# Linear attention with a relu feature map: output product turned round, with KV as the stationary operand and a transpose back in fp32

## Chip, cores, metric

One core of a Trainium2 chip. The metric is the device time of one execution in microseconds (us); several executions are taken of each kernel, each kernel beside the kernel before on the same chip. The span in a profile is shorter than the time by about 1.8 us, because it runs from the first to the last recorded instruction.

## The reference

```python
# Q, K, V: (8, 12, 512, 64) fp32
Q_feat = np.maximum(0, Q);  K_feat = np.maximum(0, K)
KV    = np.einsum('bhkd,bhkv->bhdv', K_feat, V)
K_sum = np.sum(K_feat, axis=2)
numerator   = np.einsum('bhqd,bhdv->bhqv', Q_feat, KV)
denominator = np.einsum('bhqd,bhd->bhq', Q_feat, K_sum)
return numerator / (denominator[:, :, :, None] + 1e-10)
```

There are 96 heads. The kernels take K and V in 24 groups of four heads and Q and the output in 12 "octets" of eight. Inputs are 37.7 MB, the output 12.6 MB.

## The kernel before

K, V and Q come in as bf16 (cast by the transfer). VectorE applies relu and head masks to K, V is masked by VectorE and ScalarE in halves, TensorE makes KV with the sum of K in a 65th column, ScalarE copies KV to SBUF as a block-diagonal pair of heads. Q is transposed on TensorE and put through relu by ScalarE into two buffers, padded with zeros, so that each 32-column strip of the array works for one pair of heads. The output product then has Q as the stationary operand and comes out with rows on the partitions, ready to be divided by its own 65th column.

```python
def mm_kv(g):
    ps_kv[g] = pkv.tile([P, 2, D1], fp32, name="ps_kv")          # pkv: 2 PSUM buffers
    for r in range(R):                                           # R = 16
        nc.tensor.matmul(ps_kv[g], kf[g][:, r, :, :]..., vo[g % NB][:, r, :, :],
                         start=(r == 0), stop=(r == R - 1), ...)
# ... cut ...
def mm_out(o, j):                                                # rounds of 6, 6 and 4
    # ... cut ...
    for v in range(nu):
        for z in range(2):
            for w in range(4):                                   # four 32-column strips
                nc.tensor.matmul(po[hs, b, c:c + 2 * D1],
                    qtf[o % NZ][:, z, u * P + 32 * w:u * P + 32 * w + 32],
                    kvd[(2 * o + h // 4) % NK][:, h % 4 // 2, h % 2, :, :], start=(z == 0), stop=(z == 1), ...)

def norm(o, j, o_sb):
    nc.vector.tensor_scalar(den, pv[:, :, :, D], scalar1=1e-10, scalar2=None, op0=Alu.add)
    nc.vector.reciprocal(rec, den)
    nc.vector.tensor_tensor(o_sb[...], pv[:, :, :, 0:D], rec.unsqueeze(3).to_broadcast(...), op=Alu.mult)

def cuts(o):                                                     # stores of octets 1 and 3 in pieces
    return ((16, P), (0, 5), (5, 10), (10, 15), (15, 16)) if o in (1, 3) else ((0, P),)
# ... cut: one loop over octets interleaves kv, out_round of the octet before, preparation, qt and store
```

Stores are held back on purpose: the queue that issues them first reads a bit of a K tile five octets ahead.

Of the kernel before, what the change touches and what calls it, by code (L numbers as in the profile page):

```python
# [10 lines left out]
def kernel(  # L11
# [7 lines left out]
    nc = tc.nc  # L19
    B, H, S, D = Q.shape  # L20
    assert D == 64
    P = 128
    D1 = D + 1
# [3 lines left out]
    R = S * 4 // P  # L27
    RQ = S * 8 // P
    NHG = 4
    U = RQ // 2  # L30
    NG = NH // NHG
    NO = NG // 2
# [4 lines left out]
    fp32 = mybir.dt.float32  # L37
# [4 lines left out]
    def pool(name, bufs, **kw):  # L42
        return ctx.enter_context(tc.tile_pool(name=name, bufs=bufs, **kw))
# [5 lines left out]
    kfp = pool("kfp", 4)  # L49
    rcp = pool("rcp", 4)  # L50
    outp = pool("outp", DELAY + 2)
    pkv = pool("pkv", 2, space=bass.MemoryType.PSUM)
    pqt = pool("pqt", 2, space=bass.MemoryType.PSUM)
    pou = pool("pou", 2, space=bass.MemoryType.PSUM)

    def view(X, f):
# [2 lines left out]
    Qr, Kr, Vr, Or = view(Q, RQ * D), view(K, R * D), view(V, R * D), view(out, RQ * D)  # L59

    ident = consts.tile([P, P], bf16, name="ident")
    NB = 4
    NK = 4
    NZ = 2




    vo = [consts.tile([P, R, 2, D1], bf16, name=f"vo{i}") for i in range(NB)]
    kvf = [consts.tile([P, NHG * 2 * D1], bf16, name=f"kvd{i}") for i in range(NK)]  # L70
    kvd = [x.rearrange("p (t s c d) -> p t s c d", t=2, s=2, c=2) for x in kvf]
    mask = consts.tile([P, 2, 2], fp32, name="mask")
    scratch = consts.tile([1, D], bf16, name="scratch")


    qtf = [consts.tile([P, 2, U * P], bf16, name=f"qt{i}") for i in range(NZ)]
    qtz = [x.rearrange("p z (u w y c) -> p z u w y c", u=U, w=4, y=2) for x in qtf]

    ctx.enter_context(tc.manual_schedule())

# [17 lines left out]
        nc.scalar.dma_start(out=v_sb[g].rearrange("p r d -> p (r d)"), in_=Vr[g])  # L98
    load_q(0)
    make_identity(nc, ident)  # L100
    for o in range(1, NO):
        load_kv(2 * o)
        load_kv(2 * o + 1)
        load_q(o)

    def zero(i):
        if i == 0:
            for h in range(NHG):
                for s in range(2):
                    nc.vector.memset(mask[32 * h:32 * h + 32, 0, s:s + 1], 1.0 if h % 2 == s else 0.0)  # L110
            for t in range(2):
                nc.vector.memset(mask[:, 1, t:t + 1], 0.0)
                nc.vector.memset(mask[64 * t:64 * t + 64, 1, t:t + 1], 1.0)
        if i < NB:
            nc.vector.memset(vo[i][:, :, :, D:D1], 0.0)
            for t in range(2):
                nc.vector.memset(vo[i][64 * t:64 * t + 64, :, t, D:D1], 1.0)
        nc.vector.memset(kvf[i].bitcast(fp32), 0.0)  # L118

    def zero_q(i):  # L120
        nc.vector.memset(qtf[i].rearrange("p z f -> p (z f)").bitcast(fp32), 0.0)  # L121

    kf, ps_kv, ps_qt, ps_out = {}, {}, {}, {}

    def prep(g):
        kf[g] = kfp.tile([P, R, 2, D], bf16, name="kf")
        for s in range(2):
            nc.vector.tensor_scalar(kf[g][:, :, s, :], k_sb[g], scalar1=0.0,  # L128
                                    scalar2=mask[:, 0, s:s + 1], op0=Alu.max, op1=Alu.mult)
        nc.vector.tensor_scalar(vo[g % NB][:, :, 0, 0:D], v_sb[g], scalar1=mask[:, 1, 0:1],  # L130
                                scalar2=None, op0=Alu.mult)

    def prep_act(g):
        nc.scalar.activation(vo[g % NB][:, :, 1, 0:D], v_sb[g], Act.Copy, scale=mask[:, 1, 1:2])  # L134

    def mm_kv(g):
        ps_kv[g] = pkv.tile([P, 2, D1], fp32, name="ps_kv")
        for r in range(R):
            nc.tensor.matmul(  # L139
                ps_kv[g], kf[g][:, r, :, :].rearrange("p s d -> p (s d)"), vo[g % NB][:, r, :, :],  # L140
                start=(r == 0), stop=(r == R - 1), skip_group_check=True)

    def evac_kv(g):
        for s in range(2):
            for c in range(2):
                nc.scalar.copy(kvd[g % NK][64 * c:64 * c + 64, :, s, c, :],  # L146
                               ps_kv[g][64 * s:64 * s + 64])


    def transp(o, i):  # L150
        ps_qt[o, i] = pqt.tile([P, U // 2, P], bf16, name="ps_qt")
        for u in range(U // 2):
            nc.tensor.transpose(ps_qt[o, i][:, u, :], q_sb[o][:, i * (U // 2) + u, :], ident)  # L153

    def evac_qt(o, i, eng=None):
        us = slice(i * (U // 2), (i + 1) * (U // 2))
        pv = ps_qt[o, i].rearrange("p u (w y c) -> p u w y c", w=4, y=2)
        for z in range(2):
            if eng is nc.vector:
                eng.tensor_scalar(qtz[o % NZ][:, z, us, :, z, :], pv[:, :, :, z, :], scalar1=0.0,  # L160
                                  scalar2=None, op0=Alu.max)
            else:
                nc.scalar.activation(qtz[o % NZ][:, z, us, :, z, :], pv[:, :, :, z, :], Act.Relu)  # L163


    ROUNDS = ((0, 6), (6, 6), (12, 4))

    def mm_out(o, j):
        po = pou.tile([P, 2, 512], fp32, name="ps_out")
        ps_out[o, j] = po  # L170
        u0, nu = ROUNDS[j]
        for v in range(nu):
            u, b, c = u0 + v, v // (nu // 2), v % (nu // 2) * 2 * D1
            for z in range(2):
                for w in range(4):
                    hs = slice(32 * w, 32 * w + 32)
                    h = 2 * w + z
                    nc.tensor.matmul(  # L178
                        po[hs, b, c:c + 2 * D1],
                        qtf[o % NZ][:, z, u * P + 32 * w:u * P + 32 * w + 32],  # L180
                        kvd[(2 * o + h // 4) % NK][:, h % 4 // 2, h % 2, :, :],
                        start=(z == 0), stop=(z == 1), skip_group_check=True)

    def norm(o, j, o_sb):
        u0, nu = ROUNDS[j]
        pv = ps_out[o, j][:, :, 0:nu * D1].rearrange("p b (r d) -> p b r d", d=D1)
        den = rcp.tile([P, 2, nu], fp32, name="den")
        nc.vector.tensor_scalar(den, pv[:, :, :, D], scalar1=1e-10, scalar2=None, op0=Alu.add)  # L188
        rec = rcp.tile([P, 2, nu], fp32, name="rec")
        nc.vector.reciprocal(rec, den)  # L190
        nc.vector.tensor_tensor(  # L191
            o_sb[:, 2 * u0:2 * (u0 + nu)].rearrange("p (b r) d -> p b r d", b=2),
            pv[:, :, :, 0:D],
            rec.unsqueeze(3).to_broadcast([P, 2, nu, D]), op=Alu.mult)



    def cuts(o):
        return ((16, P), (0, 5), (5, 10), (10, 15), (15, 16)) if o in (1, 3) else ((0, P),)



# [1 line left out]
    def store(o, o_sb):  # L204
        if o + DELAY < NO:
            nc.sync.dma_start(out=scratch, in_=k_sb[2 * (o + DELAY)][0:1, 0, :])
        Ov = Or[o].rearrange("p (r d) -> p r d", d=D)
        if o == NO - 1:
            for j in range(2):
                rs = slice(RQ // 2 * j, RQ // 2 * (j + 1))  # L210
                nc.sync.dma_start(out=Ov[:, rs], in_=o_sb[:, rs])
            return
        for p0, p1 in cuts(o):
            nc.sync.dma_start(out=Ov[p0:p1], in_=o_sb[p0:p1])

    zero(0)
    prep(0)
    prep_act(0)
    zero(1)
    prep(1)  # L220
    prep_act(1)
    zero_q(0)
    for k in range(2, NK):
        zero(k)
    zero_q(1)
    def kv(g):
        mm_kv(g)
        evac_kv(g)

    def qt(o):  # L230
        for i in range(2):
            transp(o, i)
            evac_qt(o, i, nc.vector if o == NO - 1 and i == 1 else None)

    def prepare(g):
        prep(g)
        prep_act(g)

    def out_round(o, j, o_sb):
        mm_out(o, j)  # L240
        norm(o, j, o_sb)



    for o in range(NO + 1):
        if o > 0:
            o_sb = outp.tile([P, RQ, D], fp32, name="o_sb", tag="o_sb")
        if o < NO - 1:
            kv(2 * o)
        if o > 0:  # L250
            out_round(o - 1, 0, o_sb)
        if o < NO - 2:
            prepare(2 * o + 2)
        if o > 0:
            out_round(o - 1, 1, o_sb)
        if o < NO - 1:
            kv(2 * o + 1)
            qt(o)
        if o < NO - 2:
            prepare(2 * o + 3)  # L260
        if o > 0:
            out_round(o - 1, 2, o_sb)
            store(o - 1, o_sb)
        if o == NO - 2:
            prepare(2 * NO - 2)
        if o == NO - 1:
            prepare(2 * NO - 1)
            kv(2 * NO - 2)
            kv(2 * NO - 1)
            qt(o)  # L270
# [1 line left out]
_INS = ['Q', 'K', 'V']  # L272
_OUTS = [((8, 12, 512, 64), 'float32')]
# [25 lines left out]
```

## Time and profile before

| | before |
|---|---|
| time, median (range) | 127.52 us (127.49 to 127.63) |
| span of the profiled run | 125.6 us |
| busy: TensorE, VectorE, ScalarE | 63%, 65%, 61% |
| memory traffic over the span | 401 GB/s |
| last Q tile landed, VectorE ended, last store landed | 111.5, 119.9, 124.7 us |

The landing times are the trace's completion records of each transfer. A digit in a row of slices is a busy share in tenths over one fortieth of the span, and 9 is 90% or more. In a row of a group the numbers after the first bar are the busy time in us and the mean duration of one instruction in ns; after the second, the idle time of the engine ahead of these instructions and what ended it. The lines themselves are in the prediction below.

### The profile page before, as it was taken

To read this page: it belongs to the slowest core of one execution; us is meant where nothing else is said; L and a number is where in the kernel's file an instruction comes from. 1 tells how busy PE (TensorE), PEld (TensorE's weight loads), DVE (VectorE), ACT (ScalarE), POOL (GpSimd) and SP (SyncE) were. 2 spreads that over 40 slices of the span, in tenths; PEclk is the share of its full clock that TensorE was granted. 3 is DMA by queue.
4 is the path that set the end of the run, shared out by engine and by line. 5 is a ranking of instruction groups with operands and counts; after the bars stand their busy time and mean duration, and the time that the engine had idled before them with its cause. 6 is when DMAs were issued, how large, how long until landed. Compare 5 with 4: busy or idle time off the path is not lost.

```text
span 125.6 us, 4876 instructions
## 1 busy us (share of the span) xinstructions
PE 78.7 (63%) x2112; PEld 69.4 (55%) x2112; DVE 81.2 (65%) x212; ACT 76.0 (61%) x167; POOL 31.7 (25%) x62
## 2 busy tenths in 40 slices
PE   0042908978398956535996697289765997558300
PEld 0041907957387845435985686287744895457200
DVE  3356785798936959674569697439628658942910
ACT  0255891599298898660899849509908959535000
POOL 6903334323243331241142133034022000000000
PEclk9999999999859999996799859959996579985995
DMA  3999999999999999999999999999999999999993
GB/s 120 378 305 210 217 204 211 217 207 219 202 215 211 208 217 320 260 216 311 270 211 296 290 211 281 296 221 231 343 223 215 328 258 213 322 419 417 407 400 153
DMA packets 10789, 32.82 MB, mean 261 GB/s; under 512 B 1424, under 2 KB 1424, under 8 KB 9360
## 3 DMA queue, kind: packets, MB, share of 16 engines
q0 software_dynamic: 8064, 17.83, 74.3%
q1 hardware_dynamic: 2416, 13.63, 27.1%
q10 hardware_dynamic: 288, 1.05, 2.1%
q8 instruction: 16, 0.26, 0.7%
q14 instruction: 5, 0.04, 0.1%
HBM read 37.75 MB, written 12.58 MB: 401 GB/s over the span
## 4 chain that ended last, share of the span: by engine, by line
DMA 32%; PE 30%; DVE 15%; issue 12%; ACT 6%; SPq 0%; ACTq 0%
DMA v_sb<-in_V_dram 25%; PE ps_out L178 14%; PE ps_kv L139 12%; DMA kv_first<-in_K_dram 7%; DVE o_sb L191 5%; PE ps_qt L153 4%; DVE kf L128 3%; DVE qt L121 3%; ACT qt L163 3%; ACT kvd L146 2%; DVE vo L130 2%; DVE rec L190 1%; ACT vo L134 1%; DVE den L188 1%; DVE kvd L118 0%
## 5 line engine op out<-in xcount | busy, mean ns | idle before, releaser
L139 PE MATMUL ps_kv<-vo,kf 128*128 128x130 bf16 x384 | 33.6, 253 | 22.2 <-ACT vo L134 10.1
L178 PE MATMUL ps_out<-kvd,qt 128*32 128x130 bf16 x1536 | 33.4, 240 | 16.1 <-issue 12.4
L139 PEld LDWEIGHTS <-kf 128*128 128x128 bf16 x384 | 28.6, 114 | 25.6 <-DVE vo L130 16.9
L178 PEld LDWEIGHTS <-qt 128*32 128x32 bf16 x1536 | 26.6, 106 | 21.6 <-issue 14.0
L146 ACT CAST kvd<-ps_kv 64x130 bf16<-64x130 f32 x96 | 25.2, 263 | 19.2 <-PE ps_kv L139 17.3
L134 ACT ACTIVATE vo<-v_sb,mask 128x1024 bf16<-128x1024 bf16 x22 | 26.2, 1190 | 10.9 <-DMA v_sb<-in_V_dram 10.7
L191 DVE TENSOR_TENSOR o_sb<-ps_out,rec 128x768 f32<-128x768 f32 (+1 forms) x36 | 31.3, 869 | 1.4
L163 ACT ACTIVATE qt<-ps_qt 128x512 bf16<-128x512 bf16 x46 | 23.8, 603 | 0.3
L128 DVE TENSOR_SCALAR kf<-k_sb,mask 128x1024 bf16<-128x1024 bf16 x44 | 19.1, 477 | 6.2 <-DMA k_sb<-in_K_dram 6.2
L85 POOL DMA_DIRECT2D k_sb<-in_K_dram x22 | 12.5, 569 | 39.5 <-DMA q_sb<-in_Q_dram 24.6
L188 DVE TENSOR_SCALAR den<-ps_out 128x12 f32<-128x12 f32 (+1 forms) x36 | 5.9, 164 | 17.8 <-PE ps_out L178 17.8
L153 PE MATMUL ps_qt<-ident,q_sb 128*128 128x128 bf16 x192 | 16.3, 251 | 1.2 <-issue 0.9
L87 POOL DMA_DIRECT2D v_sb<-in_V_dram x22 | 12.2, 555 | 16.3 <-DMA k_sb<-in_K_dram 6.7
L153 PEld LDWEIGHTS <-q_sb 128*128 128x128 bf16 x192 | 14.6, 116 | 1.4 <-issue 1.0
L130 DVE TENSOR_SCALAR vo<-v_sb,mask 128x1024 bf16<-128x1024 bf16 x22 | 10.7, 485 | 1.1 <-DMA v_sb<-in_V_dram 1.1
L190 DVE RECIPROCAL rec<-den 128x12 f32<-128x12 f32 (+1 forms) x36 | 7.9, 220 | 1.2
L91 POOL DMA_DIRECT2D q_sb<-in_Q_dram x12 | 6.5, 542 | 7.8 <-DMA v_sb<-in_V_dram 4.1
L128 DVE TENSOR_SCALAR kf<-kv_first,mask 128x1024 bf16<-128x1024 f32 x4 | 2.9, 766 | 4.6 <-DMA kv_first<-in_K_dram 4.6
L134 ACT ACT_TABLE_LOAD x1 | 1.3, 1283 | 5.5 <-DMA kv_first<-in_V_dram 5.5
L121 DVE MEMSET qt<- 128x2048 f32 x2 | 3.5, 1765 | 0.7 <-issue 0.7
L134 ACT ACTIVATE vo<-kv_first,mask 128x1024 bf16<-128x1024 f32 x2 | 2.4, 1179 | 2.7 <-DMA kv_first<-in_V_dram 2.7
L160 DVE TENSOR_SCALAR qt<-ps_qt 128x512 bf16<-128x512 bf16 x2 | 0.8, 420 | 2.9 <-PE ps_qt L153 2.9
(13 smaller groups left out, 4.9 us busy)
## 6 DMA issues: line engine op xcount, KB each, us to landing
out_dram<-o_sb SPq DMA_DIRECT2D x9, 1024.0 KB, 9.4
q_sb<-in_Q_dram POOLq DMA_DIRECT2D x12, 512.0 KB, 14.7
k_sb<-in_K_dram POOLq DMA_DIRECT2D x22, 256.0 KB, 14.0
v_sb<-in_V_dram POOLq DMA_DIRECT2D x22, 256.0 KB, 13.4
out_dram<-o_sb SPq DMA_DIRECT2D x2, 896.0 KB, 8.8
kv_first<-in_V_dram ACTq DMA_DIRECT2D x2, 512.0 KB
kv_first<-in_K_dram SPq DMA_DIRECT2D x2, 512.0 KB
out_dram<-o_sb SPq DMA_DIRECT2D x2, 512.0 KB, 4.7
```

The lines of the kernel that those rows point to most:

```text
L85: nc.gpsimd.dma_start(out=k_sb[g].rearrange("p r d -> p (r d)"), in_=Kr[g])
L87: nc.gpsimd.dma_start(out=v_sb[g].rearrange("p r d -> p (r d)"), in_=Vr[g])
L128: nc.vector.tensor_scalar(kf[g][:, :, s, :], k_sb[g], scalar1=0.0, scalar2=mask[:, 0, s:s + 1], op0=Alu.max, op1=Alu.mult)
L130: nc.vector.tensor_scalar(vo[g % NB][:, :, 0, 0:D], v_sb[g], scalar1=mask[:, 1, 0:1], scalar2=None, op0=Alu.mult)
L134: nc.scalar.activation(vo[g % NB][:, :, 1, 0:D], v_sb[g], Act.Copy, scale=mask[:, 1, 1:2])
L139: nc.tensor.matmul(ps_kv[g], kf[g][:, r, :, :].rearrange("p s d -> p (s d)"), vo[g % NB][:, r, :, :], start=(r == 0), stop=(r == R - 1), s ...
L146: nc.scalar.copy(kvd[g % NK][64 * c:64 * c + 64, :, s, c, :], ps_kv[g][64 * s:64 * s + 64])
L153: nc.tensor.transpose(ps_qt[o, i][:, u, :], q_sb[o][:, i * (U // 2) + u, :], ident)
L163: nc.scalar.activation(qtz[o % NZ][:, z, us, :, z, :], pv[:, :, :, z, :], Act.Relu)
L178: nc.tensor.matmul(po[hs, b, c:c + 2 * D1], qtf[o % NZ][:, z, u * P + 32 * w:u * P + 32 * w + 32], kvd[(2 * o + h // 4) % NK][:, h % 4 // ...
L190: nc.vector.reciprocal(rec, den)
L191: nc.vector.tensor_tensor(o_sb[:, 2 * u0:2 * (u0 + nu)].rearrange("p (b r) d -> p b r d", b=2), pv[:, :, :, 0:D], rec.unsqueeze(3).to_broa ...
```

## The change

It computes the output transposed. KV of one pair is stationary and 256 columns of transposed Q stream past it: 8 products per octet in place of 128. ScalarE copies the result to SBUF in fp32, TensorE transposes it back in fp32, and VectorE multiplies by reciprocal denominators. Those come from 16 narrow products of their own, with the entries of other heads masked out. The padded Q buffers go. VectorE takes over ScalarE's half of the V mask. In PSUM, where the kernels have TensorE's results written, two buffers for KV become two halves of one, and the transposed products and the denominators get buffers of their own (a buffer for KV or for the Q transposes is called a bank below). The cut stores go too.

```diff
-    pkv = pool("pkv", 2, space=bass.MemoryType.PSUM)
+    pkv = pool("pkv", 1, space=bass.MemoryType.PSUM)
     pqt = pool("pqt", 2, space=bass.MemoryType.PSUM)
+    pot = pool("pot", 2, space=bass.MemoryType.PSUM)
+    pde = pool("pde", 1, space=bass.MemoryType.PSUM)
     pou = pool("pou", 2, space=bass.MemoryType.PSUM)
 ... cut ...
+    ps_kv = pkv.tile([P, 2, 256], fp32, name="ps_kv")
 ... cut ...
-    def prep_act(g):
-        nc.scalar.activation(vo[g % NB][:, :, 1, 0:D], v_sb[g], Act.Copy, scale=mask[:, 1, 1:2])
+        nc.vector.tensor_scalar(vo[g % NB][:, :, 1, 2:D + 2], v_sb[g], scalar1=mask[:, 1, 1:2],
+                                scalar2=None, op0=Alu.mult)
 ... cut ...
+    def out_t(o):
+        ot[o] = otp.tile([P, U, 8, 16], fp32, name="ot_sb")
+        q = qt_sb[o % NZ].rearrange("p u (h c) -> p u h c", h=8)
+        for j in range(4):
+            ps = pot.tile([P, 2, U, 16], fp32, name="ps_ot")
+            for i in range(2):
+                nc.tensor.matmul(ps[:, i], kvd[o % NK][:, 2 * j + i, 1:2 * D + 1], q[:, :, 2 * j + i, :], ...)
+            nc.scalar.copy(ot[o][:, :, 2 * j:2 * j + 2], ps.rearrange("p h u c -> p u h c"))
+    def denom(o):
+        ... 16 products of 16 columns; VectorE: mask product, reduction, add, reciprocal
+    def out_round(o, j, o_sb):
+        ps = pou.tile([P, 8, D], fp32, name="ps_out")
+        for v in range(4):
+            nc.tensor.transpose(ps[:, 2 * v:2 * v + 2]..., ot[o][:, 4 * j + v]..., ident32)
+        nc.vector.tensor_tensor(o_sb[:, 8 * j:8 * j + 8], ps, rec[o][...]..., op=Alu.mult)
 ... cut ...
-        for p0, p1 in cuts(o):
-            nc.sync.dma_start(out=Ov[p0:p1], in_=o_sb[p0:p1])
+        nc.sync.dma_start(out=Ov, in_=o_sb)
```

The loop of the changed kernel issues, for octet o: `kv(2o)`, rounds 0 and 1 of octet o-1, `kv(2o+1)`, `qt(o)` (Q transposes and relu), rounds 2 and 3 of octet o-1, `out_t(o)`, `denom(o)`.

## The prediction

> **What bounds the kernel now.** I read the slices first, because they say whether anything but an engine is always busy, then the groups for unit costs, and then the end of the chain and the store queue, because only there does a finished time become visible.

> The page of the kernel before, its slices and the memory total:

> ```profile
> PEclk9999999999859999996799859959996579985995
> DMA  3999999999999999999999999999999999999993
> GB/s 120 378 305 210 217 204 211 217 207 219 202 215 211 208 217 320 260 216 311 270 211 296 290 211 281 296 221 231 343 223 215 328 258 213 322 419 417 407 400 153
> ...
> HBM read 37.75 MB, written 12.58 MB: 401 GB/s over the span
> ```

> The transfers are busy in all slices but the first and the last. Loads are cast from fp32 to bf16 on the way, so 210 GB/s written is 420 GB/s read: the same rate as the 419 of the last slices, which are stores alone. 50.3 MB at 420 GB/s is 120 us of the 125.6. No compute engine passes 65% of the span. So the kernel is bound by transfers, and compute matters only where it makes them wait.

> The chain that ended last and the queue that issues stores, at the end of the span:

> ```profile
> 104.43 0.69 DVE o_sb L191
> 105.12 0.79 DVE kf L128 x2
> ...
> 112.46 0.27 ACT kvd L146
> ...
> 113.61 1.09 ACT qt L163 x2
> ...
> 119.17 0.69 DVE o_sb L191
> ```
> ```profile
> 104.18 6.19 SPq L214 DMA_DIRECT2D out_dram<-o_sb  x5
> 118.85 1.37 SPq L211 DMA_DIRECT2D out_dram<-o_sb  x2
> ```

> By the landing records the last Q tile lands at 111.5 us, and V of group 23 at 107.4. VectorE ends at 119.9, the last half store goes out at about 120.2 and lands at 124.7. The stores before it land at 113.3, 116.9, 119.7, 122.2 and 123.5, one per 2.5 us for 1 MB, so transfers are still saturated there. Compute may end about 1.5 us later at no cost (the store that would land at 123.5 + 1.2 is still queued until then); beyond that each us of delay is a us of time. With an empty queue I count 4.7 us from VectorE's end to the end of the span, and 1.8 from span to time (127.4 against 125.6).

> Unit costs, from the groups with shapes kept apart:

> ```profile
> L139 PE MATMUL ps_kv<-vo,kf 128*128 128x130 bf16 x384 | 33.6, 253 | 22.2 <-ACT vo L134 10.1 <-DVE vo L130 5.3 <-issue 4.3
> L178 PE MATMUL ps_out<-kvd,qt 128*32 128x130 bf16 x1536 | 33.4, 240 | 16.1 <-issue 12.4 <-DVE o_sb L191 2.0 <-ACT qt L163 1.6
> L134 ACT ACTIVATE vo<-v_sb,mask 128x1024 bf16<-128x1024 bf16 x22 | 26.2, 1190 | 10.9 <-DMA v_sb<-in_V_dram 10.7
> L146 ACT CAST kvd<-ps_kv 64x130 bf16<-64x130 f32 x96 | 25.2, 263 | 19.2 <-PE ps_kv L139 17.3
> L163 ACT ACTIVATE qt<-ps_qt 128x512 bf16<-128x512 bf16 x46 | 23.8, 603 | 0.3
> L153 PE MATMUL ps_qt<-ident,q_sb 128*128 128x128 bf16 x192 | 16.3, 251 | 1.2 <-issue 0.9 <-DMA q_sb<-in_Q_dram 0.3
> L130 DVE TENSOR_SCALAR vo<-v_sb,mask 128x1024 bf16<-128x1024 bf16 x22 | 10.7, 485 | 1.1 <-DMA v_sb<-in_V_dram 1.1
> L191 DVE TENSOR_TENSOR o_sb<-ps_out,rec 128x512 f32<-128x512 f32 x12 | 8.3, 692 | 0.4
> L190 DVE RECIPROCAL rec<-den 128x12 f32<-128x12 f32 x24 | 5.5, 228 | 0.8
> ```

> See that an output product costs 33.4/1536 = 22 ns though one lasts 240 (four of them share the array), and that TensorE spends 17 us in "issue" gaps in front of lines 178 and 139, which cost nothing while transfers are saturated. A warm chain piece of 16 KV products takes 1.04 us (65 ns each), of 16 bf16 transposes 0.89 (56 ns).

> [...] The trace before has no fp32 on TensorE[...], and that is the weak point of this prediction.

> **The change part by part**, per octet of heads (12 in all; 8 us of loads for one before 42 us, about 10 us with stores between, from the landings).

> TensorE. Removed: 128 products x 22 ns = 2.8 us. KV products stay, 2 x 1.04. Q transposes stay, 0.89. Added: 8 products of 256 columns, estimated at 110 ns from twice 56: 0.9; 16 denominator products of 16 columns,[...] 16 x 56 ns = 0.9; 16 fp32 transposes at T each. Sum 4.8 + 16T.

> ScalarE. Removed: 2 masked V copies at 1.10 pitch = 2.2. Added: 4 copies of 512 fp32 elements[...]: 2.1. Relu becomes 2 x 0.95 in place of 4 x 0.51: 1.9. KV copies stay, 2 x 1.13. Sum 6.3, as before.

> VectorE. Added: the second V mask, 2 x 0.41; mask product and reduction over 256 elements, about 0.35 each; add 0.1; a reciprocal of 32 elements, about 0.35. Removed: 3 small adds and 3 reciprocals, 1.1 us; the normalization is 4 x 0.61 = 2.4. Sum about 6.9 (before 6.1). Removed once: clearing the padded Q buffers, 3.5.

> No engine's sum reaches 8 us unless T is over 0.2. But the parts are now in series. Before, the product after relu went straight to VectorE. Now there is a second trip through PSUM and ScalarE: KV product, KV copy, relu, transposed product, fp32 copy, fp32 transpose. ScalarE is in order, and its next KV copy stands behind the fp32 copies of this octet, and its KV product behind this octet's denominators. Counting from the end of the four fp32 copies: the last transposed products were done 0.8 us earlier, so denominators (0.9) and KV product (1.04) end at +1.3 with semaphores; then 8 transposes (8T) and the second KV product, +2.3 + 8T; its copy 1.13; relu 1.9; first products 0.4; four copies 2.1. Period p = about 8.0 + 8T (a schedule written out with these durations[...] gives 8.1 + 8T at the granted clocks seen[...]).

> The start: the second group's KV copies wait for its preparation, and the first transposed product can start at about 17.6. The last octet costs 3.6 us more than a period, since all four rounds of octet 10 stand ahead of the last preparation and of both KV products. After its transposed products, 6.4 us to VectorE's end (copies and denominators 4.0, four rounds of 0.61), then 4.7 + 1.8. Time = 17.6 + 11 x (8.1 + 8T) + 3.6 + 6.4 + 6.5 = 123.2 + 88T.

> Stores: octets 1 and 3 lose their cuts[...]. A packet of 8 KB lasts 0.32 us, so this is worth 0.6 us at most, and only if transfers stay the bound. Fewer TensorE instructions (4226 rows to 1752 in the stream) should remove most of the "issue" gaps; they lay beside other work.

> **The rivals.**
> 1. Transfers stay the bound, everything new is hidden. For it: the DMA row, and no engine over 65%. Against it: the period of 8.1 + 8T exceeds the 8 us of loads, so compute loses ground in the first 42 us and can only regain it at 10 us per octet. Needs T about 0.06, as for bf16. Time 127.5 to 129.
> 2. [...]T = 0.107. Compute falls about a us per octet behind until the stores begin, and the chain through ScalarE ends the kernel: 132.6. My choice.
> 3. [...]T = 0.107 + 0.056 = 0.16: 137.
> 4. [...]TensorE is the bound, about 159.[...]
> A gain is nearly out of reach: 50.3 MB don't move faster, and the end has some 1.5 us to give.

> **Range and chances.** Weights of about 0.22, 0.38, 0.25 and 0.1, with 0.05 for things left out, put the middle at 133. Range 128 to 146: below it only a hidden change[...]. Limit of "same" is 130.1, reached only with the first rival: 0.21. Faster than 125: 0.03. Slower: 0.76.

> **What would show it.** The group of fp32 transposes: 16 in a row give T. ScalarE's fp32 copies near 0.6 us, waiting for the transposed product; KV copies waiting for the KV product. KV products starting 9 us apart, and no longer waiting for V from memory. VectorE ending near 126, slices near the end below 400 GB/s or with transfers idle. If KV products still wait for transfers and VectorE ends by 121, the first rival holds and I am wrong about the series; if TensorE is at 90% and over, the fourth.

The sum came to 123.2 + 88T, and with T = 0.107 to 132.6, recorded as 133. No trace or run showed T when it was written, as the kernel before has no fp32 on TensorE. Measured it is 0.109 us (e3_bank, below), and the sum with it 132.8.

What the changed kernel's trace shows for the durations that were forecast, in the octet from 40.8 us: two relus 1.94 us (forecast 1.9), four fp32 copies 2.13 (2.1), four products of 256 columns 0.60 (8 in 0.9), 16 denominator products 0.43 from the first start to that of the next product (0.9), mask product 0.61 and reduction 0.42 (0.35 each), add 0.18 (0.1), reciprocal 0.35 (0.35), two rounds of the normalization 1.29 (0.61 each). From relu's end to the transposed product it takes 0.05 us (49.52 to 49.57). ScalarE's timeline has its work in the order of issue: the four fp32 copies end at 43.39 us, and only then comes the next octet's KV copy, at 44.18. In the kernel before, masked V copy and the operation after it start 1.06 us apart (28.07 and 29.13 us; forecast 1.10). A store's packet of 8 KB takes 0.32 us there (median of 1408 in the trace).

## The result, and the profile after

| | before | changed |
|---|---|---|
| time, median (range) | 127.52 us (127.49 to 127.63) | 140.61 us (139.5 to 141.1) |
| span of the profiled run | 125.6 | 138.5 |
| busy: TensorE, VectorE, ScalarE | 63%, 65%, 61% | 65%, 68%, 54% |
| last Q tile landed, VectorE ended, last store landed | 111.5, 119.9, 124.7 | 111.0, 135.0, 137.6 |

The ratio is 1.1013 (95% interval 1.0942 to 1.1084). Ratios here are the mean time of one kernel's fast runs over that of the other's of the same rounds, so not quite the ratio of the medians quoted.

The slices of the changed kernel, its traffic, and groups with shapes kept apart:

```profile
PEclk9999998698699999977999999779689999999655
DMA  4999999999999999999999999999999999170033
...
HBM read 37.75 MB, written 12.58 MB: 363 GB/s over the span
```
```profile
L202 PE MATMUL ps_out<-ident,ot_sb 128*128 128x128 f32 x192 | 31.4, 317 | 2.0 <-DVE o_sb L204 1.5 <-ACT ot_sb L178 0.5
L178 ACT COPY ot_sb<-ps_ot 128x512 f32<-128x512 f32 x48 | 25.6, 587 | 6.2 <-PE ps_ot L176 6.2
L156 ACT CAST kvd<-ps_kv 64x130 bf16<-64x130 f32 x96 | 25.3, 264 | 34.4 <-PE ps_kv L150 32.0 <-DVE rec L195 1.6
L176 PE MATMUL ps_ot<-qt,kvd 128*128 128x256 bf16 x96 | 16.4, 271 | 24.7 <-ACT qt L166 17.4 <-ACT ot_sb L178 6.0
```

The loads landed when they did before, within 0.6 us. But by then compute was behind, and the transfers ran dry: the last six slices are mostly idle. No engine is full either. ScalarE's KV copies waited 32.0 us for KV products, and TensorE's transposed products 17.4 us for relu and 6.0 for the fp32 copies: the two engines wait for each other.

TensorE's timeline of two octets, at full clock and with a stretch at half clock (granted clock 0.50 from 60.74 to 64.15 us; columns: start us, duration us, engine, source line, operation, operands and count; in brackets the idle time before it and what ended it):

```profile
49.57 0.60 PE L176 MATMUL ps_ot<-qt,kvd 128*128 128x256 bf16 x4 [1.37 <-ACT qt L166]
50.67 0.87 PE L176 MATMUL ps_ot<-qt,kvd 128*128 128x256 bf16 x4 [0.51 <-ACT ot_sb L178]
51.38 0.58 PE L185 MATMUL ps_den<-kvd,qt 128*128 128x16 bf16 x16
51.80 1.11 PE L150 MATMUL ps_kv<-vo,kf 128*128 128x132 bf16 x16
52.75 1.04 PE L202 MATMUL ps_out<-ident,ot_sb 128*128 128x128 f32 x8
54.09 1.11 PE L150 MATMUL ps_kv<-vo,kf 128*128 128x132 bf16 x16 [0.30 <-ACT kvd L156]
55.03 1.06 PE L165 MATMUL ps_qt<-ident,q_sb 128*128 128x128 bf16 x16
55.93 1.04 PE L202 MATMUL ps_out<-ident,ot_sb 128*128 128x128 f32 x8
58.34 0.60 PE L176 MATMUL ps_ot<-qt,kvd 128*128 128x256 bf16 x4 [1.37 <-ACT qt L166]
...
60.58 1.81 PE L150 MATMUL ps_kv<-vo,kf 128*128 128x132 bf16 x16
62.19 1.91 PE L202 MATMUL ps_out<-ident,ot_sb 128*128 128x128 f32 x8
...
68.27 0.60 PE L176 MATMUL ps_ot<-qt,kvd 128*128 128x256 bf16 x4 [1.37 <-ACT qt L166]
```

From one first transposed product (line 176) to the next is a period. Here they are 8.77 and 9.93 us. Over the kernel, the first one starts at 21.1 us and the periods are 9.81, 9.88, 8.78, 8.77, 9.93, 8.78, 8.77, 9.91, 9.93, 8.78 and, for the last octet, 12.82. The long ones are those with a stretch at half clock, where the first KV product and eight transposes take 1.8 to 1.9 us each in place of about 1.0. Note the wait of 0.30 us in front of the second KV product: it waits for ScalarE's copy of the first. Both go to halves of one bank; in e3_bank, where each has its own, the wait is gone.

The start, ScalarE's timeline of the changed kernel:

```profile
13.60 1.28 ACT L156 ACT_TABLE_LOAD   x1 [13.60 <-DVE kvd L132]
14.89 1.09 ACT L156 CAST kvd<-ps_kv 64x130 bf16<-64x130 f32 x4
17.99 1.09 ACT L156 CAST kvd<-ps_kv 64x130 bf16<-64x130 f32 x4 [2.00 <-PE ps_kv L150]
```

ScalarE did nothing for 13.6 us, until the KV buffer was cleared behind the second group's preparation. Then came the activation table, which the kernel before loads at 5.5 us for its V mask, then the first KV copy, and only then could the second KV product start, at 16.04 us.

### The profile page after: what moved, and what is told of

The parts are those of the page before. It is cut to its first block, busy times and chain, and to the rows that moved or that the text cites. A ratio compares the mean times of both kernels' runs of the same rounds, so it can differ in the third digit from the quotient of the medians.

```text
span 138.5 us, 2735 instructions
## 1 busy us (share of the span) xinstructions
PE 90.5 (65%) x1056; PEld 80.6 (58%) x1056; DVE 93.7 (68%) x220; ACT 75.5 (54%) x169; POOL 32.3 (23%) x65
## 3 DMA queue, kind: packets, MB, share of 16 engines
HBM read 37.75 MB, written 12.58 MB: 363 GB/s over the span
## 4 chain that ended last, share of the span: by engine, by line
ACT 40%; PE 38%; DVE 8%; DMA 6%; issue 3%; SPq 0%; ACTq 0%; DVEq 0%
PE ps_kv L150 20%; ACT qt L166 17%; ACT kvd L156 13%; ACT ot_sb L178 9%; PE ps_out L202 8%; PE ps_ot L176 7%; DMA kv_first<-in_K_dram 6%; PE ps_den L185 4%; DVE o_sb L204 2%; DVE kf L139 2%; ACT L156 1%; DVE own L188 1%; DVE vo L144 1%; DVE vo L141 1%; DVE den L191 1%
## 5 line engine op out<-in xcount | busy, mean ns | idle before, releaser
L150 PE MATMUL ps_kv<-vo,kf 128*128 128x132 bf16 x384 | 32.4, 248 | 17.0 <-DVE vo L144 9.9
L204 DVE TENSOR_TENSOR o_sb<-ps_out,rec 128x512 f32<-128x512 f32 x48 | 31.5, 687 | 8.5 <-PE ps_out L202 7.5
L202 PE MATMUL ps_out<-ident,ot_sb 128*128 128x128 f32 x192 | 31.4, 317 | 2.0 <-DVE o_sb L204 1.5
L176 PE MATMUL ps_ot<-qt,kvd 128*128 128x256 bf16 x96 | 16.4, 271 | 24.7 <-ACT qt L166 17.4
L178 ACT COPY ot_sb<-ps_ot 128x512 f32<-128x512 f32 x48 | 25.6, 587 | 6.2 <-PE ps_ot L176 6.2
L176 PEld LDWEIGHTS <-kvd 128*128 128x128 bf16 x96 | 9.4, 97 | 31.5 <-issue 30.9
L202 PEld LDWEIGHTS ps_out<-ident,ot_sb 128*128 128x128 f32 x192 | 25.8, 167 | 3.0 <-DVE o_sb L204 2.3
L188 DVE TENSOR_TENSOR own<-ps_den,mask_h 128x256 f32<-128x256 f32 x12 | 7.3, 612 | 24.0 <-PE ps_den L185 24.0
L166 ACT ACTIVATE qt<-ps_qt 128x1024 bf16<-128x1024 bf16 x24 | 23.3, 1021 | 0.3
L139 DVE TENSOR_SCALAR kf<-k_sb,mask 128x1024 bf16<-128x1024 bf16 x44 | 19.3, 480 | 0.0
L144 DVE TENSOR_SCALAR vo<-v_sb,mask 128x1024 bf16<-128x1024 bf16 x22 | 10.6, 484 | 0.0
L141 DVE TENSOR_SCALAR vo<-v_sb,mask 128x1024 bf16<-128x1024 bf16 x22 | 10.6, 480 | 0.0
L156 ACT ACT_TABLE_LOAD x1 | 1.3, 1283 | 13.6 <-DVE kvd L132 13.6
## 6 DMA issues: line engine op xcount, KB each, us to landing
v_sb<-in_V_dram POOLq DMA_DIRECT2D x22, 256.0 KB, 13.2
```

Source lines behind the costliest of these rows:

```text
L139: nc.vector.tensor_scalar(kf[g][:, :, s, :], k_sb[g], scalar1=0.0, scalar2=mask[:, 0, s:s + 1], op0=Alu.max, op1=Alu.mult)
L150: nc.tensor.matmul(ps, kf[g][:, r, :, :].rearrange("p s d -> p (s d)"), vo[g % NB][:, r, :, 1:D4 - 1], start=(r == 0), stop=(r == R - 1), ...
L156: nc.scalar.copy(kvd[g // 2 % NK][64 * c:64 * c + 64, h0 + s:h0 + 4:2, c * D1:c * D1 + D1], ps[64 * s:64 * s + 64, :, c:c + D1])
L166: nc.scalar.activation(qt_sb[o % NZ][:, us], ps, Act.Relu)
L176: nc.tensor.matmul(ps[:, i], kvd[o % NK][:, 2 * j + i, 1:2 * D + 1], q[:, :, 2 * j + i, :], start=True, stop=True, skip_group_check=True)
L178: nc.scalar.copy(ot[o][:, :, 2 * j:2 * j + 2], ps.rearrange("p h u c -> p u h c"))
```

## The experiments

The main theory is **series**: TensorE and ScalarE alternate in one chain from the first KV copy to the end, and the time is the length of that chain. Half-clock windows lengthen it, and idle stretches bring these on: that part is tested by e5_warm and e6_bf16_warm. The rivals are **TensorE throughput** (the fp32 transposes are simply too much work) and **transfers** (the form of the stores). All edits are to the changed kernel except where said otherwise. All results were correct against the reference, also those in bf16. The kernel before had medians of 127.52, 127.52 and 127.61 us in the three sets.

| run | time, median us | ratio to before (95% interval) |
|---|---|---|
| e1_start | 137.62 | 1.0806 (1.0783 to 1.0829) |
| e2_bf16 | 143.23 | 1.1228 (1.1205 to 1.1252) |
| e3_bank | 139.88 | 1.0982 (1.0939 to 1.1025) |
| e4_bank_bf16 | 130.94 | 1.0291 (1.0236 to 1.0346) |
| e5_warm | 134.89 | 1.0555 (1.0504 to 1.0605) |
| e6_bf16_warm | 134.93 | 1.0573 (1.0547 to 1.0598) |
| e7_all | 128.66 | 1.0124 (1.0063 to 1.0184) |
| e8_cuts | 141.25 | 1.1077 (1.1046 to 1.1107) |
| e9_order | 127.43 | 0.9986 (0.9972 to 0.9999) |
| e10_order_all | 127.94 | 1.0039 (1.0010 to 1.0068) |
| e11_order_all_cuts | 129.34 | 1.0137 (1.0090 to 1.0185) |
| e12_before_nocuts | 128.12 | 1.0039 (1.0026 to 1.0053) |

### e1_start: the start repaired

```diff
+    nc.scalar.activation(warm, mask_w, Act.Relu)      # tiny; loads the table at once
     zero(0)
+    zero_kv(0)
     prep(0)
     zero(1)
     prep(1)
-    zero_kv(0)
```

> The changed kernel with only its start repaired: ScalarE's table is loaded by a tiny activation at once, and the first KV buffer is cleared before the first preparation instead of after the second. Series theory (one unbroken chain of TensorE and ScalarE from the first KV copy to the end sets the time): the first transposed product moves from 21.1 us to about 18.2, all later ones with it, and the time falls by 2.5 to 3.5 us from 140.6. TensorE-throughput theory (fp32 transposes fill the engine): the same shift, as it too runs from start to end. Transfer theory (the stores' form matters): no change.

Measured: 137.62 us, 3.0 us less. The first transposed product moved from 21.1 to 18.2 us, as expected. VectorE ended 2.9 us earlier too (132.2 for 135.0), so a delay at the start is carried to the end, and two badly placed instructions cost 3 us. This speaks against transfers but doesn't separate series from throughput.

### e2_bf16, e3_bank, e4_bank_bf16: shorter transposes, a second bank, both

```diff
-        ot[o] = otp.tile([P, U, 8, 16], fp32, name="ot_sb")
+        ot[o] = otp.tile([P, U, 8, 16], bf16, name="ot_sb")       # e2, e4; ps_out and identity in bf16 too
```
```diff
-    pkv = pool("pkv", 1, ...);  pde = pool("pde", 1, ...)         # e3, e4
+    pkv = pool("pkv", 2, ...)                                     # ps_den shares the tag of ps_qt
-        ps = ps_kv[:, g % 2, 0:2 * (D + 2)]...
+        ps = pkv.tile([P, 2, D + 2], fp32, name="ps_kv")
```

> The changed kernel with the way back in bf16 (copies, identity and transposes), at some loss of precision. TensorE-throughput theory: 16 transposes at about 0.06 in place of 0.12 us save 1.0 us per octet, 11 us in all. Series theory as the trace refines it: the second KV product of each octet waits for the first one's KV copy (0.30 us in a quick octet), so shorter transposes are hidden in the octets at full clock; only octets with a throttled stretch and the last rounds gain: 1 to 3 us in all.

> The changed kernel with two PSUM banks for the KV product, as before the change; the denominators take turns in the banks of the Q transposes to make room. Series theory: the wait of 0.30 us in front of each second KV product goes, and in the first octet the second KV product starts when its data are prepared (13 us) rather than behind the first KV copy (16 us), with its copy then behind the late first copy: 2 us at the start, 0.3 in each of some 6 quick octets, 3 to 5 us in all. TensorE-throughput theory: 2 us from the start alone at most.

> Both: two banks for the KV product and the way back in bf16. Series theory: with the wait for the KV copy gone, eight shorter transposes (0.5 us) do shorten each period, so this gains 5 to 7 us over the two banks alone, more than the two parts measured alone add up to; time about 130 to 132. TensorE-throughput theory: 1.0 us per octet as with bf16 alone, and the two gains simply add.

Measured: bf16 alone 143.23 us, 2.6 us *slower*, where neither theory allowed it. The second bank alone 139.88, 0.7 us faster where 3 to 5 were expected. Both together 130.94, in the range expected, but 8.9 us faster than the bank alone where 5 to 7 were expected, and though bf16 alone lost time. Throughput can't be the bound: with half the transpose time gone (0.109 to 0.056 us each, measured below) the kernel got slower.

The misses have their answer in the clock. The clock row of bf16 alone:

```profile
PEclk9999999995995986986999779689689599955555
```

It has a half-clock window in nearly every octet: eight from 31.8 to 113.7 us, each 3.41 us long, mostly 10.24 us apart, which is three windows; the changed kernel had five up to 101.7. After the first octet its one period without such a window is 8.77 us, the same as with fp32, as the series theory says (the wait for the first KV copy hides the gain). With two banks, the wait of 0.30 us was gone, two of ten periods were free of such windows, and they took 8.31; with both edits every second one was, at 7.82 to 7.88. The first transposed product with two banks came at 18.9, 2.2 us earlier. So the terms of the theory hold, but with either edit alone the gain was paid back in half-clock windows, it seems because a quicker TensorE idles more. That was still an argument at this point; the next two runs tested it.

### e5_warm, e6_bf16_warm: unneeded work

```diff
             ps = pot.tile([P, 2, U, 16], fp32, name="ps_ot")
+            if j == 0:
+                for x in range(10):        # 12 in e6; overwritten by the products that follow
+                    nc.tensor.matmul(ps[:, x % 2]..., ident, q_sb[o][:, 2 * (x % 8):2 * (x % 8) + 2, :]..., start=True, stop=True, ...)
```

> The changed kernel with ten unneeded products of 256 columns in each octet, in TensorE's wait of 1.37 us for relu; their result is overwritten by the transposed products. Clock theory (TensorE's idle stretches bring on the half-clock windows of 3.4 us, each of which stretches an octet from 8.78 to 9.9 us): more work makes it faster; all periods near 8.8, five windows fewer at 1.1 us each and quicker last rounds, 134 to 136 us. TensorE-throughput theory: 10 products more per octet at 0.11 us add up to 1 us per octet, 145 us or more. If the windows come without regard to idling: 140 to 142.

> The way back in bf16, which alone gave 143.2, with twelve unneeded products per octet in the longer wait for relu (1.80 us). Clock theory: the loss with bf16 came from half-clock windows in nearly every octet, and goes with them: periods of 8.8 as with fp32 at full clock, because the wait for the first KV copy still sets the second KV product; 133 to 135 us. If bf16 transposes cost something by themselves (the wait of 0.32 us for VectorE in front of the second KV product): stays above 140.

Measured: 134.89 and 134.93 us, both as the clock theory had it; the granted clock of the profiled runs rose from 0.904 to 0.966 and from 0.841 to 0.959. Ten products more per octet made the changed kernel 5.7 us faster, and twelve made the bf16 version 8.3 us faster. Busy time of the engines with the unneeded work, in windows of 3.4 us of the same stretch (first the changed kernel, then e5_warm; columns: window, its length, then busy us and instruction count of TensorE, its weight loads, VectorE, ScalarE and GpSimd, then granted clock, DMA share, GB/s):

```profile
53.90:57.30 3.40, 2.88 (x40) 2.71 (x40) 3.40 (x8) 2.14 (x7) 1.22 (x4) 1.00 1.10 215
57.30:60.70 3.40, 1.74 (x27) 1.32 (x27) 2.21 (x6) 2.88 (x6) 0.43 (x1) 1.00 1.05 351
60.70:64.10 3.40, 3.40 (x28) 3.34 (x25) 2.26 (x5) 1.29 (x5) 1.06 (x2) 0.51 1.10 220
```
```profile
57.30:60.70 3.40, 2.81 (x44) 2.60 (x44) 1.97 (x6) 2.59 (x7) 0.53 (x1) 1.00 1.05 345
60.70:64.10 3.40, 3.10 (x44) 2.90 (x43) 3.29 (x8) 2.13 (x7) 1.01 (x2) 1.00 1.10 224
```

In the changed kernel a window with 1.74 us of TensorE work is followed by one at a clock of 0.51. With the filling no window between 20 and 118 us had less than 2.15, and the clock first halved at 124.2 us, in the last rounds. From the second on, all periods but the last are 8.72 to 8.78 us.

### e7_all: start, bank and filling together

The edits of e1, e3 and e5 at once.

> The changed kernel, still in fp32, with the repaired start, two KV banks and ten unneeded products per octet. Series and clock theory: first transposed product at about 18, periods of 8.3, so compute reaches the pace of the loads; the loads' last landing at 111 us sets the end as before the change: 127.5 to 130 us. TensorE-throughput theory: not below 137.

Measured: 128.66 us (one of the four runs 130.31). Periods of 8.25 to 8.31 us up to the eighth octet, then 9.06 and 10.0, about the pace at which the loads of an octet land by then. Nearly the whole loss is gone with every added operation still in place, in fp32.

### e8_cuts and e12_before_nocuts: the stores

The first puts the cut stores of octets 1 and 3 back into the changed kernel, the second takes them out of the kernel before.

```diff
-        return ((16, P), (0, 5), (5, 10), (10, 15), (15, 16)) if o in (1, 3) else ((0, P),)
+        return ((0, P),)                                          # e12, in the kernel before
```

> The changed kernel with the cut stores of octets 1 and 3 put back. Series theory: transfers have idle stretches near the end, so no change beyond 0.7 us. Transfer theory: a good part of the 13 us comes back.

> The kernel before with only the cut stores taken away, one part of the change by itself. Transfers are its bound, so up to 0.6 us slower than before (127.6 to 128.2); nothing of the 13 us comes from here.

Measured: 141.25 us, no gain, and 128.12 us, a loss of 0.5. The cuts were worth half a us in the kernel before, whose transfers are busy to the end, and nothing in the changed one, whose transfers are not. The transfer theory falls.

### e9_order: nothing but the order of issue

```diff
     rec = {}
+    prep(2); kv(0)
     for o in range(NO + 1):
-        if o < NO - 1: kv(2 * o)
+        if o < NO: kv(2 * o + 1); qt(o)
         if o > 0: out_round(o - 1, 0, o_sb); out_round(o - 1, 1, o_sb)
-        if o < NO - 2: prep(2 * o + 2)
-        if o < NO - 1: kv(2 * o + 1); qt(o)
+        if o < NO - 1: prep(2 * o + 3); kv(2 * o + 2)            # next octet's KV product
         if o > 0: out_round(o - 1, 2, o_sb); out_round(o - 1, 3, o_sb); store(o - 1, o_sb)
-        if o < NO - 2: prep(2 * o + 3)
-        ... special preparation and KV products of the last octet ...
+        if o < NO - 2: prep(2 * o + 4)
         if o < NO: out_t(o); rec[o] = denom(o)
```

> The changed kernel with nothing but the order of issue altered: the KV products of the next octet are issued ahead of this octet's transposed products, and preparations one group earlier, so that ScalarE finds KV copies to do where it waited. The same work, fp32, one KV bank, start not repaired. Series theory: the period falls from 8.8 to 9.9 us to about 7.3 (VectorE's sum), compute catches up with the loads before the end, 127.5 to 131 us. TensorE-throughput or any theory in which the added work itself is the cost: stays at 137 or above.

Measured: 127.43 us, a tie with the kernel before and 13.2 us less than the changed kernel. This is the run that settles it: the same operations on the same engines in fp32, one KV bank, start not repaired (first transposed product at 21.5 us), no filling. The first four periods are 7.1 to 7.5 us; the tenth and the four before it are 9.97 to 10.0, the pace of the loads, for which VectorE's preparations now wait (in the changed kernel only those of the first groups do). Its slices, and a line of its list of waits (us in total, times, longest):

```profile
PEclk9999999999999999999999999999999999999996
DMA  3999999999999999999999999999999999999965
...
DVE kf L139 <- DMA k_sb<-in_K_dram: 10.8, 6, 2.5
```

Transfers are busy to the end again, and the clock stays full up to the last rounds. TensorE's wait for relu in front of the transposed products, 17.4 us in the changed kernel, is not in the list of waits any more: other products now fill it. What the KV products and the earlier preparations contribute one by one wasn't tested.

### e10_order_all and e11_order_all_cuts: all repairs together

The new order with the start and bank of e1 and e3, then with the cut stores as well.

> The new order with the repaired start and two KV banks. Series theory: transfers are the bound again and set the end as in the kernel before: 127.0 to 128.5 us, a tie with it, since the bytes are the same. A gain over the order alone of 0 to 2 us.

> The same with the cut stores of octets 1 and 3 put back. In a transfer-bound kernel they should be worth up to the 0.6 us estimated from packets of 0.32 us: 0.2 to 0.6 us faster than without. If compute still sets its end: no difference.

Measured: 127.94 us, within the stated range, but 0.5 us slower than the order alone, where 0 to 2 us of gain were expected; and 129.34 us with the cuts, a miss in sign. For the first a wait is in view, from the list of waits of e10_order_all (us in total, times, longest):

```profile
PE ps_qt L165 <- DVE own L188: 15.7, 9, 3.2
```

The denominators share the banks of the Q transposes there, so these now wait for VectorE's mask product, which stands behind preparations that wait for loads; that this is the cause wasn't tested. Half-clock windows came back with it (three between 55 and 100 us). For the cuts, the six runs fall into two sets, 128.5 to 128.6 and 130.0 to 130.3; the profiled one, of the quicker set, has its last load land 0.8 us later than without the cuts. Why is left open. Neither run beats the kernel before, and no run here is clearly faster than it.

## Why the prediction was right and wrong

**Right: the bound and the mechanism.** Compute took the place of transfers as the bound through a chain in which TensorE and ScalarE alternate, with no engine full. The lines it named are there: ScalarE waiting for KV products, transfers idle near the end, KV products that no longer wait for loads (after the first two groups). e9_order shows that the order is the cost: with the same work in another order, transfers hide it.

**Right: T.** The chosen rival had 0.107 us per fp32 transpose. Eight of them in a row at full clock took 0.87 us from their start to that of the next product (in e3_bank, where nothing waits), 0.109 each; in bf16 0.056 (0.45 us for eight in e4_bank_bf16). From the timelines of e3_bank and e4_bank_bf16:

```profile
51.72 1.04 PE L200 MATMUL ps_out<-ident,ot_sb 128*128 128x128 f32 x8
52.59 1.11 PE L148 MATMUL ps_kv<-vo,kf 128*128 128x132 bf16 x16
```
```profile
49.44 0.61 PE L200 MATMUL ps_out<-ident,ot_sb 128*128 128x128 bf16 x8
49.89 1.11 PE L148 MATMUL ps_kv<-vo,kf 128*128 128x132 bf16 x16
```

The fourth rival is out (TensorE was busy for 65% of the span, not 90%), and so is the first, which needed T near 0.06. The third, 137 us, came nearer to the measured time than the chosen one, but by luck: its T of 0.16 is not what was measured (0.109). The guess on the "issue" gaps in front of TensorE's products came true (none is in the list of waits), though the count was off: with the weight loads the profile has 2112 instructions, not 1752.

**Wrong: the size.** The sum was 132.6, recorded as 133; measured 140.6, a loss of 10.1% where 4.3 was forecast. VectorE ended at 135.0, not near 126. The terms against the profiled run (140.25 us):

| term | predicted | measured | difference |
|---|---|---|---|
| first transposed product starts | 17.6 | 21.1 | +3.5 |
| ten periods | 10 x 8.96 = 89.6 | 93.3 | +3.7 |
| last period | 8.96 + 3.6 = 12.56 | 12.82 | +0.3 |
| from there to VectorE's end | 6.4 | 7.7 | +1.3 |
| to the end of the span, and to the time | 6.5 | 5.3 | -1.2 |

Two steps failed, each about half of the 7.6 us.

*The start.* The step read "the second group's KV copies wait for its preparation, and the first transposed product can start at about 17.6". It left out that the two KV products now share a bank, so that the second waits for the copy of the first, and that ScalarE, without its V mask, loads its table only when the chain needs it. e1_start takes 3.0 us of it away.

*The period.* The step "8.1 + 8T at the granted clocks seen" took the clock of the kernel before as given. At full clock the period is 8.78, better than the 8.96 predicted. But half-clock windows are not a background: the waits of the new chain bring them on (granted clock 0.904; 0.966 with the wait filled in e5_warm, 0.990 in e9_order, where other products stand in it). Five of the ten periods have one, at about 1.1 us each; the wait for the KV copy, also left out, is 0.30 of each quick one. e5_warm takes 5.7 us away by removing them. The end is the +1.3: the last transposes run at half clock in the changed kernel and still do in e5_warm (7.6). In e7_all, where the clock is full until 0.3 us after VectorE's end, the same stretch takes 6.9 us, so about 0.8 of the 1.3 goes with the clock and the rest stays open.

Together the two repairs, 3.0 and 5.7 us if they add, would leave 131.9, close to the 132.6 of the sum. That exact pair wasn't run; e7_all, which also has the second bank, gave 128.66. The tail was shorter than counted: the prediction gave 4.7 us to the end of the span with an empty queue, and it took 3.5; the last half store landed 2.6 us after its issue.

## What to carry to other kernels

When a change puts a second trip through PSUM and through an engine that works in the order of issue between two products, write out the chain over a whole period, including who shares a bank (0.30 us in each quick period here), before adding up busy times: here all sums fitted under the loads and the loss was 13 us. Then look for independent work of the next iteration to issue inside the waits; moving the KV products, with the preparations ahead of them, gave back everything (140.61 to 127.43 us). And where a faster or smaller operation makes a kernel slower, look at the granted clock first (0.841 in e2_bf16, 0.904 in the changed kernel).
